# Modulation products of a diffusion block's first norm: fp32 weights unsplit on four 32-column strips

## Chip, cores and metric

One core of one Trainium2 chip runs the whole kernel. The metric is the device time of one execution in microseconds (us), the median of several runs. The profile is one execution recorded by the hardware profiler; its span runs from the first to the last instruction.

## What is computed

One layer of a diffusion transformer on 256 latent tokens and 256 context tokens, width 2048, everything in fp32. The part that the change touches is the modulation of the first norm:

```python
mod   = silu(c)     @ w_mod + b_mod      # latent tokens: one vector of 6 * 2048
mod_c = silu(c_ctx) @ w_mod + b_mod      # context tokens
sh_a, sc_a, ... = split(mod, 6)
h  = rmsnorm(x,   norm_g[0]) * (1 + sc_a)  + sh_a
hc = rmsnorm(ctx, norm_g[0]) * (1 + csc_a) + csh_a
p, p_c = h @ w_in, hc @ w_in
```

Of `w_mod` (2048 x 12288) this first part needs the 4096 columns of the shift and the scale: two vectors (`c` and `c_ctx`) times a 2048 x 4096 matrix, 33.6 MB of weights. After it come the input projection, latent attention, a gated recurrence in both directions, the merge, the output projection and a SwiGLU feed-forward.

## The kernel before

**Splitting.** TensorE multiplies in the type fp32r in one pass. To keep fp32 accuracy nearly every operand is split into a high part H and a low part L: ScalarE casts the raw fp32 tile to fp32r (`split_w`, L100) and VectorE subtracts (L102). A product is then H·H + H·L + L·H, three fp32r matmuls. A plain fp32 matmul also exists; the profile shows each as two instructions.

**Phase 0** (L160 to L264) makes the modulation vectors and the first norm, and runs the first six projection blocks beside them, k-outer. Its pieces:

- `cst` (L164 to L169): silu of `c` and `c_ctx`, split in H and L, so four columns, repeated 32 times to fill all 128 columns of a stationary operand, for each of the 16 k-blocks.
- `load_x` (L178) loads x and the context, 2 MB each in four DMAs on SP's queue; `norm_x` (L184) squares them on ScalarE, adds the squares on VectorE (x) or GpSimd (context), and `rstd_tok` (L138) and `rstd_bcast` (L147) bring 1/rms to all partitions (tiles `ptok`, `rtok`, `dg`, `pbc`, `rb`) through two small PE steps.
- The group loop (L219): `GROUPS` says how many k-blocks of the norm's output one group makes: eight groups of 2. For a group of `nk` it loads `2 * nk` tiles `wm1` of 1 MB (L225), splits each, and runs 16 k-blocks x (H, L) matmuls of 512 columns into one PSUM bank `pm` (L233). Rows 0 to 3 of `pm` are copied to `row` (L241), turned into columns by small fp32 matmuls against `sel` (tile `pt`, L244), which also add the H and L rows, and become the scale `A1` and the shift `SH1` (L248 to L250).
- Then, for each k of the group, two loads of projection weights `wst` (L256, 256 and 128 KB, split too) and `make_h` (L194), which makes the split norm outputs `hA` (latent) and `hB` (context). Each k gives six entries of `todo`: `pre_mm` (L209), six fp32r matmuls of 256 columns into the banks `pre0` to `pre5`. The entries of one group are run after the tiles 1, 2 and 3 of the next group.

**Buffers.** Raw weight tiles have three buffers, H and L halves three each. PSUM has eight banks: `pj` four (all held by `pre`), `px` four (two held by `pre`, two for `pm`, `pt`, `ptok`, `pbc`).

**Order.** The order of the instructions on each engine and each queue is laid out when the program is built, by a scheduler with a simulated timeline (L1050); it takes what is ready in its simulation, the earlier in the program the sooner. On the chip every engine then runs its list in that order. After phase 0, `project` (L305) goes on with weight tiles of 1 MB, split in the same way.

Of the kernel before, what the change touches and what calls it, by code (L numbers as in the profile page):

```python
# [7 lines left out]
F32 = mybir.dt.float32  # L8
# [12 lines left out]
EPS = 1e-6  # L21
# k-blocks of the first norm's modulation that are made at a time
GROUPS = [2, 2, 2, 2, 2, 2, 2, 2]


@with_exitstack
def block_kernel(
# [31 lines left out]

# [1 line left out]
    ones = cp.tile([P, P], F32, name="ones")  # L61
# [15 lines left out]
    ident = c0[:, 0:128]  # L77
    sel = c0[0:4, 128:130]
    cn = cp.tile([P, 896], F32, name="cn")
# [8 lines left out]

# [1 line left out]
    def load_w(src, cols=2048):  # L90
# [25 lines left out]
    def mm3(outs, w, acts, first, last):  # L116
        """outs[i] += w^T acts[i], w = (H, L) [K, 128]; acts[i] = (H, L) [K, N]."""
        H, L = w
        seq = []
        for o, (aH, aL) in zip(outs, acts):  # L120
            seq += [(o, H, aH), (o, H, aL)]
        for o, (aH, aL) in zip(outs, acts):
            seq += [(o, L, aH)]
        for i, (o, l, r) in enumerate(seq):
            nc.tensor.matmul(o, l, r, start=(first and i == 0), stop=(last and i == len(seq) - 1))  # L125

    def mm_wide(ps, w, act, first, last):
        """ps[:, 0:T] += H^T aH + L^T aH, ps[:, T:2T] += H^T aL; w = (H, L) [K, 128], act [K, 2, T] = (aH, aL)."""
        nc.tensor.matmul(ps, w[0], act.rearrange("p e t -> p (e t)"), start=first, stop=False)  # L129
        nc.tensor.matmul(ps[:, 0:T], w[1], act[:, 0, :], start=False, stop=last)  # L130
# [7 lines left out]
    def rstd_tok(sums, n, tag):  # L138
        """1 / sqrt(mean + eps) per token, on every partition; sums: [P, T] parts of the sum of squares."""
        pt = px.tile([P, 512], F32, tag="px", name="ptok")  # L140
        for hf in range(2):
            for i, a in enumerate(sums):
                nc.tensor.matmul(pt[:, hf:hf + 1], a[:, hf * P:(hf + 1) * P], ones[:, 0:1],
                                 start=(hf == 0 and i == 0), stop=(hf == 1 and i == len(sums) - 1))
        return rstd_bcast(pt, n, tag)
# [13 lines left out]

# [1 line left out]
    sg = wk.tile([P, KD, 2], F32, tag="csig", name="csig")  # L161
    nc.scalar.activation(sg, cv, AF.Sigmoid)
    nc.vector.tensor_tensor(cv, cv, sg, op=ALU.mult)
    cst = cp.tile([P, KD, 32, 4], F32R, tag="cst", name="cst")  # L164
    clo = cp.tile([P, KD, 2], F32, name="clo")
    for s in range(2):
        nc.scalar.copy(cst[:, :, :, 2 * s], bc(cv[:, :, s], 32))
        nc.vector.tensor_tensor(clo[:, :, s], cv[:, :, s], cst[:, :, 0, 2 * s].bitcast(F32), op=ALU.subtract)
        nc.scalar.copy(cst[:, :, :, 2 * s + 1], bc(clo[:, :, s], 32))  # L169

# [32 lines left out]

    # the first projection blocks run k-outer, beside the modulation products that make their operands
    NPRE = 6
# [3 lines left out]
    def pre_mm(ws, k, b):  # L209
        mm3([pre[b][:, 0:T], pre[b][:, T:2 * T]], ws(b * P, P),  # L210
            [(hs[s][k][:, 0, :], hs[s][k][:, 1, :]) for s in range(2)], k == 0, k == KD - 1)

    load_x(xT)
    load_x(ctxT)
    norm_x(0)
    norm_x(1)
    todo = []
    k0, tile_no = 0, 0
    for nk in GROUPS + [0]:  # L219
# [3 lines left out]
        for kt in range(nt):  # L223
            if nk:
                w = split_w(load_w(wm1[tile_no]))  # L225
                tile_no += 1
                n = 256 * nk
                per = 1024 // n
                for hf in range(2):
                    for e in range(2):  # L230
                        for kk in range(per):
                            k = (2 * kt + hf) * per + kk
                            nc.tensor.matmul(pm[:, 0:n], cst[:, k], w((hf * per + kk) * n, n)[e],  # L233
                                             start=(k + e == 0), stop=(k + e == KD))
            if kt > 0 or nt == 1:
                for _ in range(min(share, len(todo))):
                    pre_mm(*todo.pop(0))
        if not nk:
            break
        row = wk.tile([4, 512], F32, tag="vn", name="row")  # L240
        nc.scalar.copy(row[:, 0:n], pm[0:4, 0:n])  # L241
        pt = px.tile([P, 512], F32, tag="px", name="pt")
# [22 lines left out]

    # lower bounds of the forget gates: softmax over the two layers, entry 0
    lbm = wk.tile([P, 2, NH], F32, tag="lbm", name="lbm")
# [10 lines left out]

# [1 line left out]
    mod2 = cp.tile([P, 4, KD], F32, name="mod2")  # L280
# [22 lines left out]

# [1 line left out]
    def project(nb, streams):  # L305
# [10 lines left out]

# [1 line left out]
    cqkv = bp.tile([P, 4096], F32R, tag="b16", name="cqkv")  # L318
# [37 lines left out]
    def hblock(h, i):  # L356
        """Projection block i (value, query, forward gate, backward gate, output gate) of an HGRN head."""
        if h == 0:
            return (3, 10, 4, 5, 11)[i]
        return 12 + 5 * (h - 1) + i  # L360

# [1 line left out]
    hgx = bp.tile([P, 4096], F32, tag="b16", name="hgx")  # L363
# [28 lines left out]
    def hgrn_head(h):  # L392
# [11 lines left out]
        def gate_chain(d, psf):  # L404
# [33 lines left out]
            nc.vector.reciprocal(rdec, dec[:, 0:4])  # L438
            # two chunks at a time, with decays counted from the border between them
            a, b = d, 1 - d  # L440
# [5 lines left out]
        def keys_t(d):  # L446
# [7 lines left out]
            S[d].append(ktn)  # L454
            # scores, transposed [s, t]
            pc = px.tile([P, 2, P], F32, tag="px", name="pc")
# [8 lines left out]
        def states(d):  # L465
            """States before each pair of chunks, decayed to the border inside the pair."""
            kt, qd, dec, ktn = S[d]
# [40 lines left out]

        # value
        psv = project(hblock(h, 0), (0, 1))  # L510
# [4 lines left out]
        later(1, value_t)  # L515
        # query
        psq = project(hblock(h, 1), (0,))
# [22 lines left out]
    for h in range(NH):  # L540
        hgrn_head(h)
        if h > 0:
            mod_job(4 if h < NH - 1 else 3)
# [1 line left out]
    aT = bp.tile([P, NH, 2, T], F32R, tag="b16", name="aT")  # L545
    sgt = []

    def gates(b):
        """Block b of the gate logits of both branches."""
        if b % 2 == 0:  # L550
# [30 lines left out]
    def att_q(p, A):  # L581
# [14 lines left out]
        A["qn"] = split_ps(pq, ("f", "kk"))  # L596
        # values of both heads, [token, 2 * 128]
        A["vs"] = vs = []
# [24 lines left out]
    def att_s(i, A):  # L623
        """Scores and softmax of head i of the pair, both blocks of queries."""
        rr = slice(64 * i, 64 * i + 64)
# [56 lines left out]

# [1 line left out]
    mg = []  # L684
# [18 lines left out]

# [1 line left out]
    # modulation vectors: gt_a * g1, g2 * (1 + sc_f), sh_f, gt_f * g3  # L705
    b2 = bm.rearrange("p (a k) -> p a k", k=KD)
# [8 lines left out]
    def gate_rows(i, tag, bufs):  # L715
        """A gate times its norm's gain, along the free dimension and on every partition; 512 columns per tile."""
        nc.vector.tensor_tensor(gts[:, i], mod2[:, 3 * i], b2[:, 2 + 3 * i], op=ALU.add)
# [13 lines left out]
    def project_tok(tiles, nk, src, first, last, lead=None):  # L731
        """Two banks [P tokens, 512]: both token halves against the columns of one chunk. With lead (a tag whose
        buffers hold the last four operand blocks), the last eight blocks go to the first half before the second."""
        ps = [pj.tile([P, 512], F32, tag="pj", name="pst") for _ in range(2)]
# [25 lines left out]
    def sqrt_table(dep):  # L760
        """Has ScalarE's square root table loaded before it is needed, after dep is there."""
        t_ = wk.tile([P, 1], F32, tag="rdec", name="tbl")
        nc.scalar.activation(t_, dep, AF.Sqrt)

    def rstd_part(i, hf):
        """1 / sqrt(mean + eps) of each token of a half, [P, 1], from the sums of squares per chunk."""
        rt = cp.tile([P, 1], F32, name=f"rt{i}{hf}")
# [67 lines left out]

# [1 line left out]
    G = [None] * NFF  # L837

    def ffn_first():
        """The first two pairs of blocks, k-outer: they start as soon as one operand block is there."""  # L840
        pss = [pj.tile([P, 512], F32, tag="pj", name=f"psf{i}") for i in range(2)]
# [94 lines left out]
def _layout(i):  # L936
# [62 lines left out]
    def quads(w):  # L999
        """[chunk of 512 columns, 4 k-blocks, P, 4 * 512]"""  # L1000
        k = w.shape[0] // 512
# [26 lines left out]
    cn[:, 898:1026] = (s >= t)  # L1028
    cn[0:2, 128] = 1.0
    cn[2:4, 129] = 1.0  # L1030
    o["consts"] = cn
# [23 lines left out]
```

## Time and profile before

| | us |
|---|---|
| median of 3 runs | 1790.29 (1787.86 to 1790.58) |
| the profiled execution: span | 1787.6 |
| TensorE busy | 1746.0 (98%) |
| VectorE busy | 1182.3 (66%) |
| ScalarE busy | 865.6 (48%) |
| GpSimd busy | 32.0 (2%) |
| DMA, mean over the span | 210 GB/s |

The profiled execution's own time is known as its span only; the median of the runs shown stands 2.7 us above it, and its fastest run 0.3 us. PE is TensorE, PEld its weight loads, DVE VectorE, ACT ScalarE, POOL GpSimd, SP the engine whose queue issues most DMAs. A row of the timeline gives the start, the length, the engine, the line and the operation of one instruction or of several that were merged (x6); starts of PE instructions are recorded, their ends modelled, so that consecutive matmuls overlap in it and the distance of their starts says more than their length. "fp32r<-f32" gives output and input types.

### The profile page before, as it was taken

The page shows a single profiled execution, that of the slowest core. Times are in us where ns is not written, and L with a number is a line of the kernel's source. Part 1 is how long each engine was busy: PE and PEld are TensorE (multiplying, and loading weights), DVE is VectorE, ACT ScalarE, POOL GpSimd, SP SyncE. Part 2 cuts the span into 40 slices and gives each one's busy share as a digit, 9 for nine tenths or more (in the row PEclk, how much of TensorE's full clock was granted, in tenths as well). Part 3 has the DMA queues.
Part 4 walks back from the last instruction along what each step waited for, and adds up shares of the span by engine and source line. Part 5 has one row for each costly group of instructions (what it writes and reads, how often), then busy time and mean ns, then how long its engine had stood idle before and what let it go on. Part 6 is the DMA issues. An engine that isn't in the chain of part 4 may idle for free.

```text
span 1787.6 us, 26992 instructions
## 1 busy us (share of the span) xinstructions
PE 1746.0 (98%) x10944; PEld 1568.0 (88%) x10944; DVE 1182.3 (66%) x1758; ACT 865.6 (48%) x1245; POOL 32.0 (2%) x31
## 2 busy tenths in 40 slices
PE   4999999999999999999999989999999999999998
PEld 3999999999999888888998888888888888888886
DVE  6886786667777766666775587777445555555556
ACT  7675633333333556556444554444444444334443
POOL 2000000000000000000110000000000000000000
PEclk9999999999999999999999989999999999999999
DMA  8885455554556555647666637877555555555563
GB/s 330 294 285 211 145 190 191 179 172 170 193 203 207 200 197 192 234 172 261 234 236 212 212 122 280 285 271 268 193 198 183 184 186 189 193 197 184 184 216 130
DMA packets 59020, 374.64 MB, mean 210 GB/s; under 512 B 6512, under 2 KB 8848, under 8 KB 15632
## 3 DMA queue, kind: packets, MB, share of 16 engines
q1 hardware_dynamic: 58032, 371.36, 59.9%
q8 instruction: 85, 1.39, 0.3%
q10 hardware_dynamic: 864, 1.57, 0.2%
q14 instruction: 39, 0.32, 0.1%
HBM read 370.79 MB, written 2.11 MB: 209 GB/s over the span
## 4 chain that ended last, share of the span: by engine, by line
PE 97%; ACT 1%; DVE 1%; DMA 0%; POOL 0%; issue 0%; DVEq 0%; ACTq 0%; POOLq 0%
PE ps L125 20%; PE pst L757 18%; PE psf L129 18%; PE psf L130 9%; PE ps L129 7%; PE psb L692 5%; PE pre L125 4%; PE ps L130 3%; PE pm L233 3%; PE psf L851 1%; PE psS L635 1%; PE po L658 1%; PE psS L632 1%; PE pv L607 1%; PE pq L591 1%; PE pk L125 1%
## 5 line engine op out<-in xcount | busy, mean ns | idle before, releaser
L102 DVE TENSOR_TENSOR wL<-raw,wH 128x1024 fp32r<-128x1024 f32 (+1 forms) x556 | 675.8, 1222 | 446.8 <-ACT wH L100 446.1
L100 ACT CAST wH<-raw 128x1024 fp32r<-128x1024 f32 (+1 forms) x556 | 573.3, 1038 | 765.7 <-PE ps L125 182.1
L129 PE MATMUL psf<-h,wH 128*128 128x512 f32 x1344 | 475.1, 399 | 0.0
L130 PE MATMUL psf<-h,wL 128*128 128x256 f32 x1344 | 377.6, 281 | 0.0
L129 PEld LDWEIGHTS psf<-h,wH 128*128 128x128 f32 x1344 | 252.5, 188 | 62.8
L125 PE MATMUL ps<-hA,wH 128*128 128x256 f32 x1312 | 254.6, 286 | 0.0
L130 PEld LDWEIGHTS psf<-h,wL 128*128 128x128 f32 x1344 | 253.9, 189 | 0.2
L125 PEld LDWEIGHTS ps<-hA,wH 128*128 128x128 f32 x1312 | 203.9, 190 | 1.2 <-issue 0.5
L125 PE MATMUL ps<-hA,wL 128*128 128x256 f32 x656 | 187.3, 286 | 0.0
L129 PE MATMUL ps<-hA,wH 128*128 128x512 f32 x512 | 184.1, 400 | 0.0
L300 DVE CUSTOM_DVE_ANT_0 raw<-raw,cb 128x2048 f32<-128x2048 f32 x64 | 146.2, 2284 | 43.3 <-DMA raw<-in_wm_dram 42.8
L757 PE MATMUL pst<-wH,gA 128*128 128x512 f32 x576 | 166.7, 389 | 0.0
L130 PE MATMUL ps<-hA,wL 128*128 128x256 f32 x512 | 144.0, 282 | 0.0
L125 PE MATMUL ps<-hB,wH 128*128 128x256 f32 x672 | 137.2, 284 | 0.0
L757 PEld LDWEIGHTS pst<-wH,gA 128*128 128x128 f32 x576 | 108.0, 188 | 22.5
L125 PEld LDWEIGHTS ps<-hA,wL 128*128 128x128 f32 x656 | 124.9, 190 | 0.5 <-issue 0.5
L129 PEld LDWEIGHTS ps<-hA,wH 128*128 128x128 f32 x512 | 96.1, 188 | 23.1 <-issue 1.3
L125 PEld LDWEIGHTS ps<-hB,wH 128*128 128x128 f32 x672 | 104.6, 190 | 0.0
L757 PE MATMUL pst<-wL,gA 128*128 128x512 f32 x288 | 101.4, 389 | 0.0
L130 PEld LDWEIGHTS ps<-hA,wL 128*128 128x128 f32 x512 | 96.6, 189 | 2.5 <-DVE mx L637 1.1
L125 PE MATMUL ps<-hB,wL 128*128 128x256 f32 x336 | 95.2, 283 | 0.0
L757 PE MATMUL pst<-wH,mg 128*128 128x512 f32 x256 | 74.4, 389 | 0.0
(433 smaller groups left out, 2266.4 us busy)
## 6 DMA issues: line engine op xcount, KB each, us to landing
raw<-in_wm_dram SPq DMA_DIRECT2D x96, 1024.0 KB, 5.0
raw<-in_wfi_dram SPq DMA_DIRECT2D x84, 1024.0 KB, 4.9
raw<-in_win_dram SPq DMA_DIRECT2D x73, 1024.0 KB, 5.0
raw<-in_wfo_dram SPq DMA_DIRECT2D x44, 1024.0 KB, 4.8
raw<-in_wbr_dram SPq DMA_DIRECT2D x16, 1024.0 KB, 5.2
raw<-in_wout_dram SPq DMA_DIRECT2D x16, 1024.0 KB, 4.8
rw<-in_wst_dram SPq DMA_DIRECT2D x16, 256.0 KB, 5.5
raw<-in_wqk_dram SPq DMA_DIRECT2D x4, 1024.0 KB, 4.8
```

The lines of the kernel that those rows point to most:

```text
L100: nc.scalar.copy(H, raw[:, o:o + n])
L102: nc.vector.tensor_tensor(L, raw[:, o:o + n], H.bitcast(F32), op=ALU.subtract)
L125: nc.tensor.matmul(o, l, r, start=(first and i == 0), stop=(last and i == len(seq) - 1))
L129: nc.tensor.matmul(ps, w[0], act.rearrange("p e t -> p (e t)"), start=first, stop=False)
L130: nc.tensor.matmul(ps[:, 0:T], w[1], act[:, 0, :], start=False, stop=last)
L233: nc.tensor.matmul(pm[:, 0:n], cst[:, k], w((hf * per + kk) * n, n)[e], start=(k + e == 0), stop=(k + e == KD))
L300: nc.vector.tensor_tensor_reduce(out=raw, in0=raw, in1=cbt[0], scale=1.0, scalar=0.0, op0=ALU.mult, op1=ALU.add, accum_out=mod2[:, i // KD ...
L591: nc.tensor.matmul(pq[:, i * T:(i + 1) * T], l, r, start=(k == 0 and i == 0 and z == 0), stop=(k == 3 and i == 1 and z == 2))
L607: nc.tensor.matmul(pv[:, i, :], ckvs[:, k, l, ts_], r, start=(i == 0 and k == 0 and z == 0), stop=(i == 1 and k == 1 and z == 2))
L632: nc.tensor.matmul(psS, qn[a][:, i * T + qb * P:i * T + (qb + 1) * P], kn[b], start=(n == 0), stop=False)
L692: nc.tensor.matmul(ps[:, br * T:(br + 1) * T], l, r, start=(br == 0 and k == 0 and z == 0), stop=(br == 1 and k == NH - 1 and z == 2))
L757: mm = nc.tensor.matmul(ps[hf], l, r, start=(k == 0 and n == 0), stop=(k == nk - 1 and n == 2))
```

## The change

Phase 0's products take the raw fp32 weights. `cst` has 32 columns per k-block, of which two hold silu(c) and silu(c_ctx) and 30 are zero; it is one GpSimd memset and one VectorE copy. The products of k-block k go to the 32 output partitions 32·(k mod 4) of `pm`, with 32 columns of the array (four strips), in fp32. `row` is copied with all its 128 partitions and `sel` has ones in rows 0, 32, 64, 96 (latent) and 1, 33, 65, 97 (context), so that the small matmuls of `pt` add up the four strips. The groups are 1, 1 and then seven times 2 k-blocks. The first tile of `wm1` is loaded ahead of x, the second between x and the context, and the norm of x stands behind the products of the first tile, that of the context behind those of the second. The other lines of the diff take comments away.

```diff
-GROUPS = [2, 2, 2, 2, 2, 2, 2, 2]
+GROUPS = [1, 1, 2, 2, 2, 2, 2, 2, 2]
...
-    sel = c0[0:4, 128:130]
+    sel = c0[:, 128:130]
...
-    cst = cp.tile([P, KD, 32, 4], F32R, tag="cst", name="cst")
-    clo = cp.tile([P, KD, 2], F32, name="clo")
-    for s in range(2):
-        nc.scalar.copy(cst[:, :, :, 2 * s], bc(cv[:, :, s], 32))
-        nc.vector.tensor_tensor(clo[:, :, s], cv[:, :, s], cst[:, :, 0, 2 * s].bitcast(F32), op=ALU.subtract)
-        nc.scalar.copy(cst[:, :, :, 2 * s + 1], bc(clo[:, :, s], 32))
+    cst = cp.tile([P, D], F32, tag="cst", name="cst")[:, 0:KD * 32].rearrange("p (k m) -> p k m", m=32)
+    nc.gpsimd.memset(cst, 0.0)
+    nc.vector.tensor_copy(cst[:, :, 0:2], cv)
...
+    ahead = [load_w(wm1[0])]
     load_x(xT)
+    ahead.append(load_w(wm1[1]))
     load_x(ctxT)
-    norm_x(0)
-    norm_x(1)
...
-                w = split_w(load_w(wm1[tile_no]))
+                raw = ahead.pop(0) if ahead else load_w(wm1[tile_no])
                 tile_no += 1
                 n = 256 * nk
-                per = 1024 // n
-                for hf in range(2):
-                    for e in range(2):
-                        for kk in range(per):
-                            k = (2 * kt + hf) * per + kk
-                            nc.tensor.matmul(pm[:, 0:n], cst[:, k], w((hf * per + kk) * n, n)[e],
-                                             start=(k + e == 0), stop=(k + e == KD))
+                per = 2048 // n
+                for kk in range(per):
+                    k = kt * per + kk
+                    nc.tensor.matmul(pm[32 * (k % 4):32 * (k % 4) + 32, 0:n], cst[:, k], raw[:, kk * n:(kk + 1) * n],
+                                     start=(k < 4), stop=(k >= KD - 4))
+                if k0 == 0:
+                    norm_x(kt)
...
-        row = wk.tile([4, 512], F32, tag="vn", name="row")
-        nc.scalar.copy(row[:, 0:n], pm[0:4, 0:n])
+        row = wk.tile([P, 512], F32, tag="vn", name="row")
+        nc.scalar.copy(row[:, 0:n], pm[:, 0:n])
...
-    cn[0:2, 128] = 1.0
-    cn[2:4, 129] = 1.0
+    cn[0::32, 128] = 1.0
+    cn[1::32, 129] = 1.0
```

## Rows read from the trace of the kernel before

**Rows 1.** Three stretches: busy us and instructions of each engine, granted clock, DMA share, GB/s.

```profile
0.00:46.50 46.50, 21.49 (x85) 17.19 (x86) 29.30 (x50) 34.08 (x52) 11.35 (x11) 1.00 0.86 327
46.50:174.30 127.80, 126.29 (x837) 115.92 (x836) 104.14 (x164) 83.58 (x121) 1.90 (x2) 0.99 0.77 273
174.30:1787.60 1613.30, 1598.25 (x10025) 1434.91 (x10024) 1048.84 (x1546) 747.92 (x1073) 18.73 (x18) 1.00 0.58 201
```

**Rows 2.** The chain that ended last, in order of time: start us, length us, what.

```profile
59.45 3.45 PE pm L233 x14
...
145.32 3.45 PE pm L233 x14
164.00 10.41 PE pre L125 x72
```

**Rows 3.** Groups of TensorE instructions, 0 to 175 us: count | busy us, mean ns.

```profile
L233 PE MATMUL pm<-wH,cst 128*128 128x512 f32 x128 | 42.3, 412 | 0.0
...
L331 PE MATMUL ss<-sq,ones 128*128 128x512 f32 x2 | 1.0, 592 | 0.0
```

**Rows 4.** Timeline of TensorE in phase 0: start us, length us, engine, line, operation.

```profile
58.40 1.05 PE L244 MATMUL pt<-c,row 4*128 4x2 f32 x8
59.38 0.73 PE L233 MATMUL pm<-wH,cst 128*128 128x512 f32 x2
...
60.42 0.63 PE L233 MATMUL pm<-wH,cst 128*128 128x512 f32 x2
60.88 0.63 PE L233 MATMUL pm<-wL,cst 128*128 128x512 f32 x2
...
171.73 0.28 PE L125 MATMUL pre<-hB,wH 128*128 128x256 f32 x1
171.85 0.28 PE L125 MATMUL pre<-hA,wL 128*128 128x256 f32 x1
```

**Rows 5.** Timeline of the start, all engines.

```profile
14.18 4.34 POOL L191 TENSOR_TENSOR acc<-acc,sqx 128x512 f32<-128x512 f32 x3 [13.73 <-ACT sqx L189]
...
16.11 1.87 PE L143 MATMUL ptok<-ones,acc 128*128 128x1 f32 x8 [16.11 <-DVE acc L191]
...
18.93 7.20 POOL L191 TENSOR_TENSOR acc<-acc,sqx 128x512 f32<-128x512 f32 x4 [0.42 <-ACT sqx L189]
20.25 0.36 ACT L157 COPY rb<-pbc 128x256 f32<-128x256 f32 x1
...
26.18 1.87 PE L143 MATMUL ptok<-ones,acc 128*128 128x1 f32 x8 [6.12 <-POOL acc L191]
...
35.05 0.36 ACT L157 COPY rb<-pbc 128x256 f32<-128x256 f32 x1
...
44.12 0.98 PE L125 MATMUL pre<-hA,wH 128*128 128x256 f32 x6
```

**Rows 6.** The splits, 0 to 166 us: count | busy us, mean ns | idle before.

```profile
L102 DVE TENSOR_TENSOR wL<-raw,wH 128x1024 fp32r<-128x1024 f32 x67 | 81.9, 1253 | 12.3 <-ACT wH L100 12.0
L100 ACT CAST wH<-raw 128x1024 fp32r<-128x1024 f32 x67 | 67.8, 1046 | 33.6 <-PE pm L233 24.4 <-DMA raw<-in_wm_dram 5.0 <-DVE wL L102 2.7
```

**Rows 7.** What SP's queue waited for, 0 to 180 us: total us, times, longest.

```profile
SPq L92 <- DVE wL L102: 89.9, 31, 5.7
```

**Rows 8.** One stretch of the start, columns as in rows 1.

```profile
35.00:45.00 10.00, 9.03 (x44) 6.83 (x43) 9.20 (x15) 8.24 (x13) 0.00 (x0) 1.00 1.01 410
```

**Rows 9.** Timeline around the first plain fp32 matmul of 512 columns.

```profile
174.49 1.02 PE L331 MATMUL ss<-sq,ones 128*128 128x512 f32 x2
...
174.95 0.68 PE L125 MATMUL ps<-hA,wL 128*128 128x256 f32 x1
...
175.47 0.40 PE L125 MATMUL ps<-hA,wH 128*128 128x256 f32 x2
```

**Rows 10.** Timeline of TensorE where products of 64 rows follow those of 128.

```profile
612.47 0.49 PE L635 MATMUL psS<-spH 64*128 64x512 f32 x1
612.81 0.39 PE L635 MATMUL psS<-spL,spH 64*128 64x512 f32 x1
```

## The prediction, made before the run

> **What bounds the kernel now.** I read three stretches first [rows 1]. After 174 us TensorE is busy 99% of the time and the DMA engines 58%; nothing of the change lies there, so an earlier or later end of phase 0 moves the whole rest by the same amount. From 46.5 to 174.3 TensorE is busy 126.3 of 127.8 us, at a granted clock of 0.99. Before 46.5 it is busy 21.5 us only: it waits for data. The chain of waits shows the stretch between as a beat: the products `pm` of a group begin at 59.45 and, five groups on, at 145.32, so 17.17 us apart, and the last projection products end at 164.00 + 10.41 = 174.4 us [rows 2]. The beat is TensorE's work alone. A pair of `pm` matmuls starts 0.46 to 0.47 us after the one before, so one of 512 columns costs 0.233; a projection matmul of 256 columns costs 0.12; the eight small ones of `pt` 0.98 [rows 4]. A group is 32 x 0.233 + 72 x 0.12 + 0.98 = 7.5 + 8.6 + 1.0 = 17.1 us. There are 256 `pm` matmuls in all (128 with H, as many with L) [rows 3]. So phase 0 is a late start and then a full TensorE, and two numbers decide: when the first projection product can run (44.1 us now [rows 5]), and what TensorE has left to do from there.
>
> **Start.** The splits of the weights are gone: 64 of the 67 casts and subtractions of those rows, 1.05 us of ScalarE and 1.25 of VectorE each [rows 6]. Both lie beside TensorE in the beat and give nothing there. What they do hold is the loads: SP's queue waited 89.9 us, in 31 waits, for a subtraction to set a raw buffer free [rows 7]. After the change a buffer comes free when its products have run; `pm` being first in the program, that is soon at the start. Four ScalarE casts for `cst`, of 512 columns each, become a small memset and a copy. They ran while x was still landing, so I count nothing for them; were ScalarE what holds the squares of x, it would be a gain of up to four casts, under 4.2 us by the 1.05 of 1024 columns.
>
> The loads: 1 MB of weights now goes ahead of x, and 2 MB ahead of the context. At the 410 GB/s of a stretch with all DMA engines busy [rows 8] that is 2.6 us later for x, 5.1 for the context. Moved past on SP are the four DMAs of x (by one issue) and the four of the context (by two), about 0.4 us each, inside that. The context decides: GpSimd added its squares from 14.18 to 26.13 us, 11.5 us of work, only then could `ptok` run on TensorE, and 1/rms of the context was there at 35.4. For x the same steps, from `ptok` to the end of `rb`, took 16.11 to 20.61, 4.5 us; for the context 9.2, since TensorE, working in order, had `pm` matmuls between [rows 5]. With the additions beginning between 14.2 (no delay, since ScalarE was what held them) and 19.3 (all of it), I take 17: they end at 28.5, 1/rms is there at 33 and, with a scaling and an activation of 0.5 us each and some queueing, the first projection product runs at **35.5 us**, against 44.1. The bounds are 33 and 40.
>
> Why it can be that early although the group's vectors were late before: a first group of one k-block needs two tiles, not four, and no splits. Behind the wait for the context's `ptok` on TensorE stand the next groups' products, if the scheduler has put them there. By 35.5 us the queue can have brought 6 to 8 of the 32 weight tiles (35.5 us at 327 to 410 GB/s, less 5.6 MB for x, context, constants and first projection weights). I take seven: both groups of one and three quarters of the next, so **6.25 groups' products are left**; the bounds are 6 and 7.
>
> **What is left for TensorE from there.** 576 projection products at 0.12 are 69.1 us; `pt` 6.2 (as many instructions as before, 0.98 per group; they read 128 rows in place of 4, and a weight load of either is hidden); the last group's wait for its vectors 1.5, as between `pt` and 164.00 now. With 35.5 this makes 112.3 us, to which the products come.
>
> **The products.** Not in the trace: plain fp32 on a strip of 32 columns. Nearest is a plain fp32 product on the whole array: two instructions, from 174.49 to 175.47 with one 256-column matmul in it, so 0.98 - 0.12 = 0.86 us, 0.43 for each pass [rows 9]. Where there were two matmuls of 0.233 for a k-block (0.47), there is now one product of 0.86 that uses a quarter of the array. Everything hangs on how much of four neighbours runs at once: all (0.21 each), none (0.86). The break-even against 174.4 is at (174.4 - 112.3 - 3.8) / 100 = 0.58 us for each of the 100 products left (3.8 are the switches below).
>
> I take the middle, from the order of starts. The matmul behind the second pass is recorded at 174.95, while the second pass had still to stream until about 175.35; but the second pass itself began, the two lasting 0.59 us each and 1.02 together, only at 174.92, when the first had streamed [rows 3, 9]. The products alternate strips only after both passes of one. If starts stay in program order, a strip's second pass holds up the next strip until the first is through, and the next strip's first pass then runs beside that second pass: two at a time. A run of n products takes (n + 1) x 0.43 us. By the program the 16 products of a group come as runs of 8, 4 and 4 between projection products: 3.87 + 2.15 + 2.15 = 8.2 us. The Trainium skill ("TensorE: Matmul & The Clock Gate", Part 3) says that matmuls start and end in strict program order, which is what this case assumes.
>
> Each run also changes the way the array is divided, twice. Where products of 64 rows follow those of 128, the first after the change shows 0.49 us against 0.39 for the next [rows 10]: 0.1 us for a change. Six of them are 0.6 us a group. The Trainium skill ("TensorEngine Tiling (Array Packing)", Key Properties) has a rule that speaks against the change here: switching the tiling mode drains the engine. The row agrees that it costs, 0.1 us; no run yet shows it for columns.
>
> So a group costs 8.8 us, 6.25 groups 55, and phase 0 ends at 112.3 + 55 = 167.3, **7.1 us earlier**: span 1780.5, and with the 2.7 us that the median stands above the profiled span, **1783 us**. If 7 groups are left (+6.6) or the first product runs at 40 (+4.5), this becomes no change or a small loss; at 33 with 6 groups left, 1778. Its own range is 1776 to 1797.
>
> **Rivals.** *All four strips at once.* Then a run of 8 takes 4 x 0.43, one of 4 takes 0.86: 3.4 us a group, 4.0 with the switches, 25 in all. The shorter run covers less of the way from `pt` to the next norm outputs, for which I add 1 us for each of six groups. End at 112.3 + 25 + 6 = 143.6, 31 us earlier, 1759. The loads allow it: 4.2 MB of weights and 0.8 of projection weights take 12.1 us at 410 GB/s, the group then 14.7. For it: strips have their own columns and outputs, and 174.95 shows one instruction waiting in the engine. Against: the second pass did not start early in the same rows. The Trainium skill (the tiling page, Key Properties) has tiles executing in parallel; by that this rival is the outcome.
>
> *None at once, slower.* The place is the same, the price 0.86 us a product: 14.4 a group with switches, 90 in all, end at 202.1, 28 us later, 1818. It decides from 0.58 us a product up, as worked out. For it: in rows 9 nothing of plain fp32 overlaps anything. Against: nothing there uses part of the columns.
>
> *Two at once, but in broken runs.* The scheduler already puts `pm` pairs between projection products. In runs of two a run takes 3 x 0.43: 10.3 us a group, with a switch for each product 11.9, 74 in all, end at 187, 12 us later, 1803.
>
> **How the numbers follow.** Two at a time 0.40, all four 0.32, none 0.20, broken runs 0.08. A measurement here tells about 0.2% (3.6 us) from no change. Of the first case, whose centre is 7 us and whose start is uncertain by several, 0.28 lies below that, 0.07 within, 0.05 above; all four is faster; the other two slower. Faster 0.60, same 0.07, slower 0.33. The range takes in the first case, all four and the broken runs, 1752 to 1805, and leaves out 0.2.
>
> **What would show it.** Right: fp32 `pm` passes whose starts lie in pairs of two strips about 0.43 us apart, the beat near 18.5 us in place of 17.17, the first `pre` product at 33 to 40 us, and SP's waits for `wL` gone. All four: the beat at 13 to 15 us with gaps in TensorE. None: a beat of 24. Wrong altogether: phase 0 held by something else, as the loads with three raw buffers that now wait for TensorE, a lower granted clock in the beat, or GpSimd's additions holding the first product past 44 us.

## The result, and the profile after

The changed kernel takes **1775.38 us** in the median (1774.59 to 1775.53, 4 runs), against 1789.76 for the kernel before in the same comparison: a ratio of 0.9921, 95% interval 0.9909 to 0.9933. Forecast were 1783 us and a range of 1752 to 1805. Time and direction hold; the mechanism does not, and that the time came near the forecast is in part luck: the outcome has the products of the rival with all four strips at once, and about half of the time that they were to give was not there.

The profile after, stretches as in [rows 1] (busy us and instructions of PE, PEld, DVE, ACT, POOL, granted clock, DMA share, GB/s):

```profile
0.00:46.50 46.50, 23.26 (x153) 14.93 (x156) 18.04 (x44) 19.54 (x37) 9.97 (x12) 0.85 0.80 305
46.50:174.30 127.80, 120.33 (x911) 92.21 (x911) 52.68 (x116) 42.04 (x76) 1.89 (x2) 0.97 0.77 283
...
33.00:36.00 3.00, 3.00 (x21) 1.22 (x21) 1.32 (x5) 0.51 (x1) 0.00 (x0) 0.50 0.07 22
...
160.00:1773.40 1613.40, 1598.34 (x10025) 1436.00 (x10024) 1048.63 (x1546) 747.41 (x1073) 19.59 (x18) 1.00 0.58 201
```

All of the gain is in phase 0. What follows it is the same 1613.4 us (1613.3 before, from 174.3) with the same 10025 TensorE instructions. Two things in the rows matter below: the column of the granted clock has 0.50, its lower level of 1.2 GHz, from 33 to 36 us, and VectorE's busy time in the second stretch fell from 104 to 53 us.

One beat of the chain of waits after, from a group's last products over two runs of `pt` (start us, length us, what), which answers to [rows 2]:

```profile
98.04 1.00 PE pm L229 x8
99.04 0.79 PE pre L125 x5
99.83 1.04 PE pt L242 x8
...
101.29 0.50 DVE xt L196
...
101.81 0.52 ACT hA L197
...
102.37 0.98 PE pre L125 x6
103.34 0.99 PE pm L229 x8
104.34 5.11 PE pre L125 x41
109.44 1.00 PE pm L229 x8
110.44 2.70 PE pre L125 x21
113.14 1.04 PE pm L229 x8
...
114.26 0.59 ACT row L239
...
114.90 1.07 PE pt L242 x8
```

From `pt` to `pt` it is 15.07 us; from the second `pt` at 40.41 to the last at 145.16 there are seven beats of 14.96, where there were seven of 17.25 (40.69 to 161.44). A run of four products takes 1.00 us, switch included, 4.0 a group in place of 7.5. But the chain is no longer TensorE alone: between `pt` and the next products stand VectorE and ScalarE (`xt`, `hA`), and at times ScalarE's copy `row` stands ahead of `pt`.

The phase ended at 174.4 us and now ends at 160.1. The 14.3 us are made of the beats, 7 x (17.25 - 14.96) = 16.0; the start, 0.3 (the first beat begins at 40.4 in place of 40.7); and the end, -2.0 (from the last `pt` to the last projection product 14.95 us in place of 12.97). So the reorder at the start, which was to bring 8.6 us, brought nothing, and the end became longer. Both showed in the timeline. First the start (bracket: idle time before, and what ended it):

```profile
18.85 9.71 POOL L189 TENSOR_TENSOR acc<-acc,sqx 128x512 f32<-128x512 f32 x7 [17.59 <-ACT sqx L187]
...
28.61 1.86 PE L143 MATMUL ptok<-ones,acc 128*128 128x1 f32 x8 [8.16 <-POOL acc L189]
...
38.16 1.69 PE L125 MATMUL pre<-hA,wH 128*128 128x256 f32 x12
```

TensorE sits idle 8.2 us for GpSimd's sum of the context's squares, then works at a granted clock of 0.50, and the first projection product comes at 38.2, earlier than 44.1 [rows 5] but with only two groups of one k-block behind it. And the end:

```profile
142.63 1.99 ACT L100 CAST wH<-raw 128x1024 fp32r<-128x1024 f32 x2
...
144.53 0.57 ACT L239 COPY row<-pm 128x512 f32<-128x512 f32 x1
...
147.03 1.22 DVE L102 TENSOR_TENSOR wL<-raw,wH 128x1024 fp32r<-128x1024 f32 x1
148.18 1.67 DVE L196 SCALAR_TENSOR_TENSOR xt<-xt,A,rb 128x256 f32<-128x256 f32 x4
148.69 0.51 ACT L197 ACTIVATE hA<-xt,SH 128x256 fp32r<-128x256 f32 x1 [2.18 <-DVE xt L196]
```

The last products ended at 142.95, the first projection product of the last group starts at 149.25: 6.3 us, where it was 4.8 before the change (159.24 to 164.00). Ahead of the copy on ScalarE, and ahead of the scaling on VectorE, stand splits of raw tiles: weights of the next phase. TensorE runs projection products in part of that time; idle behind `pt` it is for 3.0 us in place of 1.5. What follows the idle time is slow as well (columns as in [rows 1]):

```profile
149.20:152.00 2.80, 2.75 (x13) 2.75 (x14) 2.22 (x6) 1.19 (x3) 0.52 (x2) 0.50 1.02 424
```

At that clock the projection products start 0.21 us apart, not 0.12, and the last 72 take 10.86 us. In the kernel before they took 10.41 [rows 2], with a granted clock of 0.53 from 164 to 166 us. So the 2.0 us of the end are 1.5 of idle time and 0.45 of this.

### The profile page after: what moved, and what is told of

Same layout as the page of the kernel before. It is cut to its first block, busy times and chain, and to the rows that moved or that the text cites. A ratio compares the mean times of both kernels' runs of the same rounds, so it can differ in the third digit from the quotient of the medians.

```text
span 1773.4 us, 26824 instructions
## 1 busy us (share of the span) xinstructions
PE 1727.6 (97%) x10976; PEld 1529.9 (86%) x10976; DVE 1109.1 (63%) x1696; ACT 800.8 (45%) x1178; POOL 31.4 (2%) x32
## 4 chain that ended last, share of the span: by engine, by line
PE 96%; DMA 1%; DVE 1%; ACT 1%; issue 0%; POOL 0%; SPq 0%; DVEq 0%; ACTq 0%
PE ps L125 20%; PE pst L755 18%; PE psf L129 18%; PE psf L130 9%; PE ps L129 7%; PE psb L690 5%; PE pre L125 4%; PE ps L130 3%; PE pm L229 2%; PE psf L849 1%; PE psS L633 1%; PE po L656 1%; PE psS L630 1%; PE pv L605 1%; PE pq L589 1%; PE pk L125 1%
## 5 line engine op out<-in xcount | busy, mean ns | idle before, releaser
L102 DVE TENSOR_TENSOR wL<-raw,wH 128x1024 fp32r<-128x1024 f32 (+1 forms) x492 | 597.1, 1216 | 450.3 <-ACT wH L100 449.4
L100 ACT CAST wH<-raw 128x1024 fp32r<-128x1024 f32 (+1 forms) x492 | 508.5, 1037 | 743.1 <-PE ps L125 182.1
```

The lines of the kernel that those rows point to most:

```text
L100: nc.scalar.copy(H, raw[:, o:o + n])
L102: nc.vector.tensor_tensor(L, raw[:, o:o + n], H.bitcast(F32), op=ALU.subtract)
```

## Experiments

Theory S: the four strips run at once, and that alone shortens the beat. Rival R: the gain comes from the splits that are gone and from the reordered start. In the edits below, everything not shown is as in the kernel named. The kernel before took 1789.76 us beside the first row, 1789.54 beside the next four, 1790.19 beside the four after them and 1788.92 beside the last three; each ratio is to its own.

| kernel | median us | ratio to before, 95% interval |
|---|---|---|
| changed kernel | 1775.38 | 0.9921 (0.9909 to 0.9933) |
| one strip | 1838.18 | one run |
| two strips | 1787.61 | one run |
| strips, old start | 1767.82 | 0.9875 (0.9861 to 0.9890) |
| split products, new start | 1789.53 | 1.000 (0.999 to 1.001) |
| changed, sums on VectorE | 1768.19 | 0.9879 (0.9865 to 0.9894) |
| changed, next splits last | 1772.67 | 0.9903 (0.9888 to 0.9918) |
| changed, old groups | 1769.06 | 0.9884 (0.9870 to 0.9899) |
| strips, old start, next splits last | 1766.16 | 0.9869 (0.9853 to 0.9886) |
| the same with sums on VectorE | 1764.49 | 0.9860 (0.9842 to 0.9877) |
| changed, old groups, sums, next splits | 1764.32 | 0.9860 (0.9844 to 0.9877) |
| the same, chain covered | 1758.26 | 0.9828 (0.9812 to 0.9843) |

### How many strips run at once

The changed kernel with S = 1 or 2 in place of 4, `row` having 32·S partitions:

```diff
-nc.tensor.matmul(pm[32 * (k % 4):32 * (k % 4) + 32, 0:n], ..., start=(k < 4), stop=(k >= KD - 4))
+nc.tensor.matmul(pm[32 * (k % S):32 * (k % S) + 32, 0:n], ..., start=(k < S), stop=(k >= KD - S))
-sel = c0[:, 128:130]
+sel = c0[0:32 * S, 128:130]
```

One strip:

> All 16 products of a group on one strip, the rest as in the changed kernel. Theory S (the four strips run at once, and that shortens the beat): a run of four products takes 4 x 0.86 us and a switch, about 3.5 in place of 1.0; the beat of a group rises from 15.0 us by four times 2.5 to about 25, phase 0 ends some 70 to 75 us later, time about 1848. Rival R (the gain comes from the splits that are gone and the earlier start; the strips don't matter): beat 15, time about 1776.

Two strips:

> Products on two strips in turn. Theory S with passes that wait at their own strip: a run of four products takes 2 x 0.86 plus a switch, 1.85 us, a beat of about 18.4 less what the longer run covers of the wait for the norm outputs (up to 1), time 1790 to 1800. Forecast's rule (passes start in program order, so a strip's second pass holds up the next strip): 5 x 0.43 plus a switch, 2.25 us, for four strips as for two; two strips would then be as fast as four. Rival R: time about 1776.

The chain of waits with one strip, then with two:

```profile
91.71 0.98 PE pt L242 x8
92.69 10.42 PE pm L229 x24
...
109.05 3.55 PE pm L229 x8
115.67 0.98 PE pt L242 x8
```

```profile
91.83 0.98 PE pt L242 x8
92.81 5.27 PE pm L229 x24
...
104.03 1.84 PE pm L229 x8
108.92 0.98 PE pt L242 x8
```

A run of four products takes 3.55 us on one strip, 1.84 on two, 1.00 on four. The beats are 23.96, 17.09 and about 15.0. A group's 16 products come in runs of 12 and 4 here, 13.97 and 7.11 us in all; with four strips they come in four runs, 4.0 us. From one strip to two the beat falls by 6.9, all that the products give; from two to four it falls by 2.1 where they give 3.1, so that about 1 us of the beat is something else from there on. Rival R falls: with the splits gone and the new start, one strip is 62.8 us slower than four. The run with one strip was 10 us below what S expected: I had added the whole 2.5 us per run to a beat that held about 1 of waiting, in each of seven beats; the rest of the 10 is not traced. The one with two strips stands 2 us below its range; its products took 7.1 us a group, where I had counted 4 x 1.85 = 7.4.

That two strips should be as fast as four falls too. The weight loads show why, first one strip, then two, then four (start us, length of all, count):

```profile
108.97 0.14 PEld L229 LDWEIGHTS pm<-raw,cst 128*32 128x32 f32 x2
109.43 0.11 PEld L229 LDWEIGHTS pm<-raw,cst 128*32 128x32 f32 x1 [0.32 <-issue]
109.86 0.11 PEld L229 LDWEIGHTS pm<-raw,cst 128*32 128x32 f32 x1 [0.32 <-issue]
```

```profile
103.95 0.14 PEld L229 LDWEIGHTS pm<-raw,cst 128*32 128x32 f32 x4
104.41 0.12 PEld L229 LDWEIGHTS pm<-raw,cst 128*32 128x32 f32 x2 [0.31 <-issue]
104.84 0.12 PEld L229 LDWEIGHTS pm<-raw,cst 128*32 128x32 f32 x2 [0.31 <-issue]
```

```profile
103.27 0.16 PEld L229 LDWEIGHTS pm<-raw,cst 128*32 128x32 f32 x8
```

With one strip two passes' loads go at once and then one each 0.43 us; with two strips four, then two each 0.43; with four strips all eight of a run within 0.16 us. The starts of the passes themselves say the same: of the eight that were loaded at 103.27, four start by 103.29 and four from 103.73 to 103.75. I read this as one pass of each strip that streams and one that waits at that strip, and the wait does not hold up the other strips.

### The parts apart

The changed kernel with the old start:

```diff
-GROUPS = [1, 1, 2, 2, 2, 2, 2, 2, 2]
+GROUPS = [2, 2, 2, 2, 2, 2, 2, 2]
-    ahead = [load_w(wm1[0])]
+    ahead = []
     load_x(xT)
-    ahead.append(load_w(wm1[1]))
     load_x(ctxT)
+    norm_x(0)
+    norm_x(1)
...
-                if k0 == 0:
-                    norm_x(kt)
```

> The four strips alone: groups of two k-blocks throughout, x and context loaded first, both norms ahead of the products, as before the change. Theory S: the beat stays at 15.0; the first projection product falls back from 38 towards 42 to 44 us, so 2 to 6 us slower than the changed kernel, 1778 to 1782. Rival R: most of the 14 us is lost, 1786 to 1790.

The other half, on the kernel before: the same lines the other way round, its products with split weights left as they are.

> The reorder alone: split weights and fp32r products as before, with groups 1, 1, 2 and so on, the first tile ahead of x, the second ahead of the context, norms behind the first two tiles. Theory S: the beat stays at 17.2, the first projection product comes 2 to 6 us earlier, 1784 to 1788. Rival R: 1776 to 1780.

The reorder alone is worth nothing, 1789.53 against 1789.54 us: its beat is 17.17 as before (`pt` at 93.21, 110.38, 127.55), its second `pt` at 43.9 stands later than the first one of the kernel before (40.7). Its first projection product does come 3.0 us earlier, at 41.1, but with the vectors of a single k-block made by then. The strips alone are worth 22 us, and the reorder then takes 7.6 back. This I had not expected: I had the strips alone slower than the whole change. The chain of waits with the old start:

```profile
52.23 0.79 PE pt L241 x8
53.02 1.85 PE pm L230 x16
...
66.11 0.79 PE pt L241 x8
...
79.98 0.79 PE pt L241 x8
...
93.99 0.92 PE pt L241 x8
```

Its first `pt` is at 34.56 us and its first projection product at 38.23, as in the changed kernel (38.16). By then it has the products of a group and a quarter, the changed kernel those of two groups of one, which make one. Its second `pt` at 52.23 stands 2.4 us ahead of the changed kernel's third (54.65). Three beats of 13.9 follow, 3.4 us less than the changed kernel takes for them, with nothing but TensorE in the chain: 4.0 + 8.6 + 1.0 = 13.6 by the terms. In them two runs of products stand right behind `pt`, 1.85 us at 53.02, which covers the 1.5 us from `pt` to the next norm output; the next two beats, with one run of 1.0 there, are 15.0, as in the change.

Which half of the reorder costs, the groups or the order of loads and norms:

```diff
-GROUPS = [1, 1, 2, 2, 2, 2, 2, 2, 2]
+GROUPS = [2, 2, 2, 2, 2, 2, 2, 2]
...
-                if k0 == 0:
+                if k0 == 0 and kt < 2:
                     norm_x(kt)
```

> The changed kernel with eight groups of two k-blocks; the loads and norms in the new order. If the small first groups are what costs the 7.6 us between the strips alone (1767.8) and the whole change (1775.4), this stands near 1768. If it is the order of loads and norms, it stands at 1774 or more, since the first group then needs four tiles of which two come behind the context.

1769.06 us: the groups of one k-block are what costs. Timeline, first and last run of `pt`:

```profile
33.43 1.25 PE L242 MATMUL pt<-c,row 128*128 128x2 f32 x8
...
137.35 0.95 PE L242 MATMUL pt<-c,row 128*128 128x2 f32 x8
```

The first `pt` of a group of two runs at 33.4, hardly later than that of a group of one (32.5), because what it waits for on TensorE is the context's `ptok`, not its weight tiles. With groups of one, two of them must pass before the seven full beats begin at 40.4; here seven beats begin at 33.4.

### The wait at the start

The changed kernel with the context's sums on VectorE:

```diff
-        eng = nc.vector if s == 0 else nc.gpsimd
+        eng = nc.vector
```

> The changed kernel with the context's squares added by VectorE in place of GpSimd. Theory N (TensorE's first projection product waits for the context's norm, that is for GpSimd's additions, which end at 28.6): the additions end with the squares, at about 23.5, the first projection product moves from 38.2 to 33 or so, TensorE's idle stretch from 20.5 shortens by 5 us; 4 to 6 us faster than the changed kernel, 1770. Rival L (the loads hold the first groups whatever the norm does): within 1 us of 1775.

1768.19 us, 7.2 faster than the change. Timeline and chain of waits of this kernel:

```profile
24.35 1.86 PE L143 MATMUL ptok<-ones,acc 128*128 128x1 f32 x8 [3.87 <-DVE acc L189]
...
33.04 2.05 PE L125 MATMUL pre<-hA,wH 128*128 128x256 f32 x12
```

```profile
42.80 7.15 DMA raw<-in_wm_dram
```

The sum of the context's squares is ready 4.3 us earlier and the first projection product runs at 33.0. TensorE's idle stretch is 3.9 us in place of 8.2. So GpSimd's additions were the term: the second `pt` comes 4.8 us earlier (35.65 for 40.41) and the phase ends 7.0 earlier (153.1); the other 2.2 arise behind it, in the beats and at the end, and were not expected. That the loads come next shows in the chain, which waits for one from 42.8 to 49.9.

### The wait at the end

In the changed kernel, the next phase's splits are queued behind `last_h`, the last instructions of `make_h` on ScalarE and VectorE:

```diff
-        w = split_w(load_w(win[nb - NPRE]))
+        raw = load_w(win[nb - NPRE])
+        with tc.issue_after(last_h[0].ins), tc.issue_after(last_h[1].ins):
+            w = split_w(raw)
```

> The changed kernel, with the splits of the next phase's weights queued behind the last norm outputs on ScalarE and VectorE. Theory W (in the last group the way from the products to the first norm output takes 6.3 us, 142.95 to 149.25, because ScalarE and VectorE first split weights of the next phase): the way shrinks to about 2.5 us, 3 to 4.5 us faster, 1771 to 1772. Rival: the wait comes from the projection weights' load or from TensorE, nothing changes, 1775.

The same on the strips with the old start:

> The strips with the old groups, loads and norms (1767.8), with the next phase's splits queued behind the last norm outputs. Theory W: from the last products to the first norm output took from 134.9 plus 1.2 to 141.7 there, of which 2.5 us are needed: 3 to 4 us faster, 1764 to 1765. Rival: 1768.

The chain of waits of the first of the two, at the end of phase 0:

```profile
145.18 0.80 PE pt L244 x8
...
147.48 10.29 PE pre L125 x72
```

From the end of `pt` to the first projection product there are now 1.5 us, as before the change, where there were 3.0. The phase ends at 157.8 in place of 160.1; 0.6 of that is the last 72 products, 10.29 us in place of 10.86. Expected were 3 to 4.5 us: the wait ahead of `pt` had been filled by projection products, which had to run anyway, all but 0.27 us of it. In the medians it is 2.7 us, with intervals that overlap a little. On the old start it is 1.7 in medians from different comparisons; there the chain shows the shorter wait (1.5 us) and a phase that ends at 150.4 in place of 153.2, while the time, above the 1764 to 1765 expected, is inconclusive.

### Together

To the strips with the old start and the next splits last, and to the changed kernel with the old groups, this line is added; to the latter also the edit of the next splits:

```diff
-        eng = nc.vector if s == 0 else nc.gpsimd
+        eng = nc.vector
```

> Strips, old groups, loads and norms, the context's squares added by VectorE, the next phase's splits behind the last norm outputs. Theory N: with x and context first, the additions end at 17 to 18 in place of 22.5, but the first group's fourth weight tile still lands at about 32 to 33, so the loads hold the first projection product and little is gained over 1766.2: 1764 to 1766.

> Strips, old groups, the new order of loads and norms, the context's squares added by VectorE, the next phase's splits behind the last norm outputs. The kernel with the new loads and old groups took 1769.1; the splits are worth about 2.5 here (from pt to the first norm output 4 us, 1.5 needed), the additions 2 to 4 (they held TensorE from 24.7 to 28.8; the fourth tile is there about then): 1763 to 1765.

1764.49 and 1764.32 us, as expected: with the sums off GpSimd the order of the loads makes no difference.

The last experiment takes up the part of a beat that is not TensorE's work, 15.0 less 13.9 us by the beats of the old start. The changed order has at most 0.79 us of projection products between the last products and `pt`, and one run of products behind `pt`, 1.0 us, for a chain of 1.5.

In the second of these two, with `mm` for the last product and `ptm` for the matmuls of `pt`:

```diff
-            if kt > 0 or nt == 1:
+            if nk:
+                share = max(len(todo) - 12, 0) if kt == 0 else 3
+            with ExitStack() as es:
+                if nk and kt == nt - 1:
+                    es.enter_context(tc.issue_after(mm.ins))
+                if kt == 0 and ptm:
+                    es.enter_context(tc.issue_after(ptm[-1].ins))
                 for _ in range(min(share, len(todo))):
                     pre_mm(*todo.pop(0))
```

> The one before, with 12 projection products of a group queued behind the group's last modulation products and up to 18 behind the small matmuls of pt, so that TensorE has work while the row is copied and the norm outputs are made. Theory C (the beat of 15.0 us is 13.7 of TensorE's work, that is 4.0 + 8.6 + 1.0, and 1.3 of waiting for this chain): the beat falls to 13.7 to 13.9, five or six beats by 1.1 each, 5 to 7 us faster than the one before. Rival D (the loads, busy 0.9 of the time, set the beat of 15): no faster.

1758.26 us, 6.1 faster than the one before it and 30.7 faster than the kernel before (1788.92 in that comparison), the best version here. Its chain of waits:

```profile
59.60 0.79 PE pt L251 x8
...
63.46 7.71 DMA raw<-in_wm_dram
...
74.62 0.80 PE pt L251 x8
...
79.01 7.49 DMA raw<-in_wm_dram
...
89.96 0.79 PE pt L251 x8
...
118.01 0.79 PE pt L251 x8
...
131.92 0.80 PE pt L251 x8
```

Of the seven beats the first two (from 31.83 and 45.69) and the last two take 13.9 us, the fifth 14.1, with TensorE alone in the chain from 45.69 on where the loads are ahead; where the chain waits for a load (63.5 to 71.2 and 79.0 to 86.5) the beat is 15.0 and 15.3. So theory C holds for five beats, and D for the third and fourth. The end gained too: 12.1 us from the last `pt` to the end of the phase, in place of 13.0 in the kernel without the cover, and here the granted clock stays at 1.00 there.

## Why the prediction was right, and where it was wrong

**The frame held.** The rest after phase 0 moved as a whole (1613.4 against 1613.3 us), the beat was the unit to count in, and its other terms, 8.6 for the projection products and 1.0 for `pt`, add up with the products to 13.6, where the beats of TensorE alone took 13.9. The sign for the loads came too: SP's queue waited 2.9 us for a subtraction to free a buffer for a weight tile of 1 MB, in place of 89.9 [rows 7]; it now waits 52.5 for products.

**The step that failed** is the one on the order of starts: "a strip's second pass holds up the next strip until the first is through". It was read from two matmuls on the whole array [rows 9], where there are no strips. On strips the second pass waits at its own strip: eight weight loads within 0.16 us, starts of four passes and four 0.45 us apart, and 1.00 us for a run, not 2.15 and two switches of 0.1. A group's products cost 4.0 us, as the first rival had them, and the Trainium skill's rule that tiles execute in parallel ("TensorEngine Tiling (Array Packing)", Key Properties) was the right one to follow; the trace agrees, at 3.55, 1.84 and 1.00 us. The Trainium skill's rule that matmuls start in strict program order ("TensorE: Matmul & The Clock Gate", Part 3) is neither borne out nor refuted by this trace, which gives the eight starts of a run, four from 103.27 and four from 103.73, but not the product that each belongs to; it did not bound what ran at once in the way that I took from it.

**The beat of that rival** was forecast at 14.7 and came at 15.0; its 1 us for a shorter cover measured 1.1 (15.0 less the 13.9 of the beats of TensorE alone), and the covered version took it away where the loads allowed it.

**The start** was mis-sized. Forecast were a first projection product at 35.5 us and 6.25 groups left; measured 38.2 and seven. The additions ended at 28.56 as forecast (28.5), by luck: they began at 18.85, not 17, and took 9.7 us, not 11.5. What came behind took 9.6 us in place of 7: `pbc` of the context was again split by products on TensorE (31.92 and 35.96), at the lower clock, which the sum did not have. And the step "a first group of one k-block needs two tiles, not four" did not matter, because the tiles were not what was late: groups of two get their `pt` at 33.4. The reorder is worth 0.0 us alone and costs 6 to 8 with the strips.

**The end** I took as unchanged, 1.5 us of idle time behind `pt`. It was 3.0, with `row` and the scaling behind splits for the next phase on engines that I had counted as free. And the sum was 1.8 us short from the outset: it priced the last 72 projection products at 0.12 us each, 8.6 in all, where [rows 2] has 10.41 for them; after the change they took 10.86. That the split weights "lie beside TensorE in the beat and give nothing" was true; that the same engines, once freed, would be given later work ahead of the chain was not seen.

The errors had opposite signs, the products too dear, the start and the end too cheap; it is by this that the time came within 8 us of the forecast. Against the rival's 143.6 the phase ended at 160.1; against the forecast's 167.3 it was 7.2 earlier. The break-even of 0.58 us for a product was too high, since it held the start's gain: with two strips a product takes 0.46 us, the beat is 17.09 against 17.17, and the time, 1787.61, is about that of the kernel before.

**Switches** cost a little less than the row for 64 rows said, 0.1 us each: the two passes of a run stream for 0.86 us, and the run takes 0.99 to 1.00, so 0.14 for the two switches of a run. There are four runs in a group, not three.

## What to carry to other kernels

Small stationary operands in plain fp32 can be put on strips of the array and run together: four products of 32 columns took 1.00 us, where they took 3.55 on one strip. When a stage has lost its bound, look at the in-order engines that were given time, since the scheduler fills them with later work that then stands ahead of the chain. And a smaller first piece only helps if the piece is what is late.

## What the runs showed that I had not expected

Each strip takes in two passes, as I read the loads one that streams and one that waits, so a pair of fp32 passes on one strip does not block its neighbours (weight loads of 8, 4 and 2 at once with four, two and one strips).

TensorE ran at half its rate for most of the start, and the column of the granted clock does not show all of it. In the changed kernel 16 passes of 256 columns at 7.69 us took 1.94 us, where the strips with the old start took 1.85 for 16 passes of 512 columns at 53.0; yet the clock's column has 1.00 at 7.69. The trace's records of the clock begin only later, at 20.65 us in the changed kernel, at 33.87 in that with the sums on VectorE, at 34.42 in the kernel before, and the column has 1.00 where there is no record. In the changed kernel the records give 0.50 from 24.1 to 37.7 us, from the idle stretch of 20.5 to 28.6 on. The kernel before was as slow at its start: two `pm` matmuls at 29.79 took 0.87 us, where two take 0.46 later. So in a start a time for matmuls has to be taken from rows of that start, by the distance of their starts.

At the end of the phase an idle stretch cost more than its length: the last 72 projection products took 10.41 us in the kernel before and 10.86 in the changed one, behind 1.5 and 3.0 us of idle time and with the granted clock at about 0.5 in their first stretch, where 72 in the beat take 8.6. With the chain covered the granted clock stayed at 1.00 there.
